# A two-layer hybrid decoder step: the matmul engine's order is fixed by the program, and the small work is cut into stages that leave at counts of big matmuls

## The chip, the cores and the metric

The kernel runs on one core of one Trainium2 chip. Its time is the device time of one execution in microseconds (us); the number to compare is the median of the runs. The engines are named as in the profile: PE (TensorE, matmuls), PEld (PE's weight loads, which run beside its matmuls), DVE (VectorE), ACT (ScalarE), POOL (GpSimd) and SP (SyncE, which here only issues DMAs).

## The reference, cut to what matters

One inference step of two identical layers for 512 prompt tokens and 8 x 4 sample tokens, together 544 token columns, with a model width of 1024:

```python
h = rmsnorm(x, norm1_g) * (1 + mod[:, 1]) + mod[:, 0]      # mod = silu(c) @ w_ada + b_ada, six sections
z = h @ w_in                                               # one projection for four mixers and the gates
yA = pool_mixer(...)       # causal window means, small linear map
yB = retention(...)        # 4 chunks of 128, two pairs of heads
yC = short_conv(...)
yD = rwkv7_mixer(...)      # serial state over the tokens: S = S * w + (S a) b + v k
proj = einsum('btnc,ncd->btnd', stack([yA, yB, yC, yD]), w_br)
x = x + mod[:, 2] * (sum(sigmoid(gates) * proj) @ w_out)
h2 = rmsnorm(x, norm2_g) * (1 + mod[:, 4]) + mod[:, 3]
up = causal_dwconv(h2 @ w_up);  x = x + mod[:, 5] * ((silu(up[:, :2816]) * up[:, 2816:]) @ w_down)
```

After the second layer comes a last rmsnorm. The mixers' states before and after the step are inputs and outputs.

## The kernel before, in words

**Big matmuls.** Activations lie with channels on the 128 partitions and the 544 tokens along the free axis, in two halves of 272. All weights of a layer come as 138 units of 128 x 1024, each loaded by one DMA into a buffer `raw` (three of them) and split into a high part `whi` (ACT, L109) and a remainder `wlo` (DVE, L110). `mm3` makes each product of a 128 x 128 weight tile with 272 tokens of three matmuls (L129, L130, L131); `unit` calls it eight times for one 128-row output of one half, so a unit has 24 big matmuls per half. The results stand in three PSUM buffers `pd`.

**Small work.** Everything else on PE writes one of five PSUM buffers `pm`. It comes from Python generators: `rwkv` (front part, then the scan of 16 chunks of 32 tokens, then the sample tokens and a group norm), `retention` (twice), `ada` (the conditioning `mod`: L191 matmuls on weights that arrive by DMA `in_wada`, layer 0 in `raw` buffers, layer 1 in the large `t4` buffers), and the norms (`rstd_of`, `norm_half`). A chunk of the scan is a serial chain over three engines:

- G: `psG`, L597, then an ACT copy to `gs` (L572);
- S: `psS`, L577, then copies into `Z` by DVE and ACT (L579, L580);
- P: `psP`, L604 (64 x 64 tiles), and `pY`, L608 (128 x 64 tiles), then DVE L616 and L622, which make the next chunk's `Z`.

Every second chunk also has V, `newZ`, L563. `psP` and `pY` do not wait for each other; `pY` feeds only an output.

**What sets the order.** The generators are advanced with `adv` and `tick`, about once per unit of big matmuls, and a `yield` covers a whole chunk. This order in the program is only a priority: the scheduler of the framework orders every engine's queue anew, PE's too, by when it thinks operands are ready. Once built, each engine works through its queue in order and waits at semaphores. The 13248 big and 1836 small matmuls in the built program are the same before and after. Before, PE's queue has 261 stretches of small matmuls, each between big ones (or at an end of the program).

Of the kernel before, what the change touches and what calls it, by code (L numbers as in the profile page):

```python
# [24 lines left out]
NU = 138  # L25
KAPPA = -math.exp(-0.5)
# [16 lines left out]
def tile_hybrid_step(ctx: ExitStack, tc: tile.TileContext, io: dict):  # L43
# [81 lines left out]
    def mm3(ps, w, s, x, first, last):  # L125
        hi, lo = w
        a, b = hi[:, s * 128:(s + 1) * 128], lo[:, s * 128:(s + 1) * 128]
        xh, xl = x
        PE.matmul(ps, lhsT=a, rhs=xh, start=first, stop=False)  # L129
        PE.matmul(ps, lhsT=a, rhs=xl, start=False, stop=False)  # L130
        PE.matmul(ps, lhsT=b, rhs=xh, start=False, stop=last)  # L131

# [47 lines left out]
    def ada(l, sec, ns, load):  # L180
# [3 lines left out]
        nxt = load(0)  # L184
        yield
        for k in range(8):
            raw = nxt
            if k < 7:
                nxt = load(k + 1)
            for n in range(4):  # L190
                PE.matmul(ps[32 * n:32 * n + 32, 0:W], lhsT=sc[:, k, :], rhs=raw[:, W * n:W * n + W], start=(k == 0), stop=(k == 7))  # L191
            yield
        sb = ZR(W)
        S.copy(sb, ps[:, 0:W])
        pt = PM()
# [8 lines left out]
        yield  # L204
# [15 lines left out]
    def adv(g, n=1):  # L220
        for _ in range(n):
            if next(g, StopIteration) is StopIteration:
                return

    bg, ticks = [], [0]

    def tick():
        ticks[0] += 1
        for every, first, g in bg:
            if ticks[0] >= first and ticks[0] % every == 0:  # L230
                adv(g)

# [13 lines left out]
    def rstd_of(accs):  # L246
# [31 lines left out]
    def norm_half(xt, half, acc, sA, shA, hh):  # L278
        c0, c1 = HS[half]
        rs = rstd_of([acc])[0]  # L280
        yield
        for k in range(8):
            u = ZR(HALF)
            V.tensor_tensor(out=u, in0=xk(xt, k)[:, c0:c1], in1=rs, op=MUL)
            modulate(u, k, half, sA, shA, hh)
            yield

    def norm_final(xt, half, acc):
        c0, c1 = HS[half]
        rs = rstd_of([acc])[0]  # L290
        yield
        for k in range(8):
            x = xk(xt, k)[:, c0:c1]
            V.scalar_tensor_tensor(out=x, in0=x, scalar=pars[0][:, P_FG + k:P_FG + k + 1], in1=rs, op0=MUL, op1=MUL)
            if k % 2:
                nc.sync.dma_start(io["o_y"][:, k - 1:k + 1, c0:c1], xt[k // 4][:, k % 4 - 1:k % 4 + 1, c0:c1])
            yield

    def both_halves(run, norm):

        ng = None
        for half in range(2):
            acc = None
            for m in range(8):
                acc = sum_sq(acc, run(m, half))
                if ng:
                    adv(ng, 2 if m else 1)
            if ng:
                adv(ng, 100)
            ng = norm(half, acc)  # L310
# [28 lines left out]
    def ln_bones(src_halves, n, scale, bias, out, floor=None):  # L339

        for c0, c1 in ((0, HALF), (HALF, TOK)):
# [15 lines left out]
    def rwkv(l, za, zb, M, yD):  # L357
# [9 lines left out]
        yield  # L367
        for T in range(5):
            n = 128 if T < 4 else 32
            psu = PM()  # L370
            PE.matmul(psu[0:n, 0:256], lhsT=th[0:65, T * 128:T * 128 + n], rhs=lora[0:65, 0:256], start=True, stop=True)
            S.activation(sig[0:n, T, :], psu[0:n, 0:256], AF.Sigmoid)
        yield
# [6 lines left out]
        yield  # L380
        rss = []
        for p in range(2):
            sq = ZR(TOK)
            S.activation(sq, za[:, 2 + p, :], AF.Square, scale=par[:, P_KK + p:P_KK + p + 1])
            rs = ZR(TOK)
            ln_bones(sq, TOK, None, None, rs, floor=1e-24)
# [5 lines left out]
        yield  # L392
# [6 lines left out]
        yield  # L399
# [39 lines left out]
        yield  # L439
        for T in range(5):  # L440
# [14 lines left out]
            S.copy(BK[:, 4 * T:4 * T + nch, :, :].rearrange("r c p t -> r (c p t)"), psB[:, 0:nch * 128])  # L455
            for c in range(nch):
                for p in range(2):
                    cc = (c * 2 + p) * 64
                    for q in range(2):
                        r = par_rows(q)  # L460
                        PE.matmul(psA[kv_rows(q), cc:cc + 64], lhsT=bkv[r, p, c].rearrange("r w t -> r (w t)"),  # L461
                                  rhs=LG[q][r, 4 * T + c, p, :], start=True, stop=True)
            mc = C_MSK if T < 4 else C_MSS
# [6 lines left out]
            yield  # L470

        for p in range(2):
            for c0, c1 in HS:
                ps = PM()
                PE.matmul(ps[:, :HALF], lhsT=lora[:, 512 + 128 * p:640 + 128 * p], rhs=za[:, 1, c0:c1], start=True, stop=True)
                S.copy(kkb[:, p, c0:c1], ps[:, :HALF])
            rk = ZR(TOK)
            V.tensor_tensor(out=rk, in0=zb[:, p, :], in1=za[:, 2 + p, :], op=MUL)
            for c0, c1 in HS:
                ps = PM()  # L480
                PE.matmul(ps[:, :HALF], lhsT=M["rkb"][:, p, :], rhs=rk[:, c0:c1], start=True, stop=True)
                V.tensor_tensor(out=kkb[:, 2 + p, c0:c1], in0=ps[:, :HALF], in1=zb[:, 2 + p, c0:c1], op=MUL)
        yield

        scr1 = drp.tile([64, 32, 32], F32, tag="scr1", name=nm("scr1"))
        scr2 = drp.tile([64, 16, 2, 32], F32, tag="scr2", name=nm("scr2"))
        for q in range(2):
            r0 = 64 if q == 0 else 0
            for p in range(2):
                nc.sync.dma_start(scr1[(2 * q + p) * 16:(2 * q + p) * 16 + 16].rearrange("c s t -> s c t"),  # L490
                                  LG[q][r0:r0 + 32, 0:16, p, 0:32])
        zaf = za.rearrange("p a b -> p (a b)")
        Nb = zaf[:, 0:1024].rearrange("p (s t) -> p s t", t=32)
        X = zaf[:, 1024:1536].rearrange("p (s t) -> p s t", t=32)
        tm = zaf[:, 1536:2048].rearrange("p (s t) -> p s t", t=32)
        nc.sync.dma_start(Nb[0:64], scr1)
        nc.sync.dma_start(Nb[64:128], scr1)
        nc.sync.dma_start(X, io["xinit"])

# [7 lines left out]
        An = ZR(64)  # L507
        IA = ZR(64)
        I2 = ZR(64)
        psN = PM()  # L510
        XTs = M["xts"]
        for q in range(2):
# [6 lines left out]
                            in1=idb, op=ADD)  # L519
            for p in range(2):  # L520
                PE.matmul(psN[rr, 32 * p:32 * p + 32], lhsT=An[rr, 32 * p:32 * p + 32], rhs=LG[q][rr, 16, p, 0:32],
                          start=True, stop=True)
            V.tensor_tensor(out=I2[rr].rearrange("r (p t) -> r p t", p=2), in0=psN[rr, 0:64].rearrange("r (p t) -> r p t", p=2),
                            in1=idb, op=ADD)
        psX = PM()
        for p in range(2):
            for q in range(2):
                r0 = 64 if q == 0 else 0
                PE.matmul(psX[32 * q:32 * q + 32, 32 * p:32 * p + 32], lhsT=IA[r0:r0 + 32, 32 * p:32 * p + 32],
                          rhs=I2[r0:r0 + 32, 32 * p:32 * p + 32], start=True, stop=True)  # L530
        V.tensor_copy(XTs[0:64].rearrange("r p t -> r (p t)"), psX[0:64, 0:64])
        yield
        for s in range(31):
# [4 lines left out]
            if s in (7, 14, 21):  # L538
                yield
# [8 lines left out]
        yield  # L548
        yield
# [20 lines left out]
        def ginv_sa(psG, xt, Zc):  # L570
            gs = M["pool"].tile([64, 2, 64], F32, tag="gs", name=nm("gs"), bufs=2)
            S.copy(gs.rearrange("r p i -> r (p i)"), psG[0:64, 0:128])  # L572
            psS = PM()
            for p in range(2):
                for q in range(2):
                    r0 = 64 if q == 0 else 0
                    PE.matmul(psS[r0:r0 + 32, 64 * p:64 * p + 64], lhsT=xt(q, p), rhs=gs[32 * q:32 * q + 32, p, :],  # L577
                              start=True, stop=True)
            V.tensor_copy(Zc[0][64:96], psS[64:96, 0:128].rearrange("r (p i) -> r p i", p=2))  # L579
            S.copy(Zc[1][0:32], psS[0:32, 0:128].rearrange("r (p i) -> r p i", p=2))  # L580

        yv = zb[:, 0:2, :]
        Z = newZ(0, 2)
# [3 lines left out]
        for T in range(4):  # L587
            psY = PM()
            pY = psY[:, 0:256].rearrange("p (q x) -> p q x", q=2)
            for c in range(4):  # L590
                ch = 4 * T + c
                if c % 2 == 0:
                    Zn = newZ(ch + 2, 2 if ch < 14 else 1)
                psG = PM()
                for p in range(2):
                    for q in range(2):
                        PE.matmul(psG[32 * q:32 * q + 32, 64 * p:64 * p + 64], lhsT=LG[q][:, ch, p, 0:32],  # L597
                                  rhs=Z[q][:, c % 2, p, :], start=True, stop=True)
                ginv_sa(psG, lambda q, p: XT[32 * q:32 * q + 32, ch, p, :], [Z[0][:, c % 2], Z[1][:, c % 2]])
                psP = PM()  # L600
                for p in range(2):
                    for q in range(2):
                        r = kv_rows(q)
                        PE.matmul(psP[par_rows(q), 64 * p:64 * p + 64], lhsT=BK[r, ch, p, :], rhs=Z[q][r, c % 2, p, :],  # L604
                                  start=True, stop=True)
                for p in range(2):
                    for q in range(2):
                        PE.matmul(pY[par_rows(q), p, 32 * c:32 * c + 32], lhsT=Z[q][:, c % 2, p, :], rhs=LG[q][:, ch, p, 32:64],  # L608
                                  start=True, stop=True)
# [883 lines left out]
```

## Time and profile before

| | us |
|---|---|
| median of 3 runs | 1999.32 |
| lowest and highest run | 1997.35, 1999.36 |
| the profiled execution, its time | 1997.68 |
| its span in the trace | 1995.9 |
| PE busy in it | 1962.4 |
| DVE, ACT, POOL busy | 1047.5, 829.4, 318.8 |

The trace records the fp32 small matmuls as two instructions each, so a group of four in the program is eight in the trace. The recorded duration of a matmul overlaps that of the next one; what a matmul costs is the distance between starts. In rows of the timeline the columns are start in us, duration in us, engine, line, operation, output<-inputs, shape and count, and in brackets the engine's idle time before, with what ended it.

### The profile page before, as it was taken

The numbers are of one execution on the slowest core, as the hardware profiler recorded it, in microseconds if no ns is written. First come the engines' busy times: TensorE is split into PE (matmuls) and PEld (weight loads), VectorE is DVE, ScalarE is ACT, GpSimd is POOL, SyncE is SP. The second block draws the span as 40 slices with busy tenths as digits, with TensorE's granted clock in tenths as the row PEclk, the third lists the DMA queues.
The fourth block names the chain that finished last, engine by engine and source line by source line (L and its number), as shares of the span: only waits on it lengthen the run. The fifth ranks groups of instructions, "written<-read, shape, count | busy, mean of one in ns | idle before, by whom it ended". The sixth has DMA issues, their size and how long they took to land.

```text
span 1995.9 us, 40151 instructions
## 1 busy us (share of the span) xinstructions
PE 1962.4 (98%) x16868; PEld 1850.0 (93%) x16868; DVE 1047.5 (52%) x2017; ACT 829.4 (42%) x1546; POOL 318.8 (16%) x589
## 2 busy tenths in 40 slices
PE   6999999999999999999999999999999999999997
PEld 5999987889999999999999999888999999999997
DVE  4465723443466553555564657344445666555665
ACT  4553322253346442434345533223444565243542
POOL 1110022213001210112202101322120022011210
PEclk9999999999999999999999999999999999999999
DMA  7314423333533443534433223223124132222231
GB/s 308 107 65 128 130 96 129 119 126 114 181 111 107 154 164 128 201 127 160 136 111 95 67 86 88 65 87 111 65 85 160 62 96 86 91 90 85 86 103 46
DMA packets 75557, 227.23 MB, mean 114 GB/s; under 512 B 20208, under 2 KB 23072, under 8 KB 73584
## 3 DMA queue, kind: packets, MB, share of 16 engines
q1 hardware_dynamic: 69872, 210.43, 31.5%
q0 software_dynamic: 3536, 11.53, 1.6%
q10 hardware_dynamic: 1968, 2.69, 0.5%
q8 instruction: 133, 2.18, 0.4%
q14 instruction: 48, 0.39, 0.1%
HBM read 213.33 MB, written 9.06 MB: 111 GB/s over the span
## 4 chain that ended last, share of the span: by engine, by line
PE 95%; DVE 2%; ACT 1%; DMA 1%; issue 0%; ACTq 0%; SPq 0%; DVEq 0%
PE pd L129 28%; PE pd L131 27%; PE pd L130 27%; PE pm L191 2%; PE pm L604 1%; PE pm L608 1%; PE pm L597 1%; PE pm L577 1%; DMA t<-in_wada 1%; PE pm L453 0%; PE pm L563 0%; PE pm L343 0%; PE pm L165 0%; PE pm L461 0%; PE pm L672 0%
## 5 line engine op out<-in xcount | busy, mean ns | idle before, releaser
L129 PE MATMUL pd<-t,whi 128*128 128x272 f32 x4200 | 1227.8, 293 | 5.0 <-ACT t L354 3.5
L131 PE MATMUL pd<-t,wlo 128*128 128x272 f32 x4200 | 1220.6, 291 | 0.0
L130 PE MATMUL pd<-t,whi 128*128 128x272 f32 x4200 | 1214.1, 289 | 0.5 <-DVE t L355 0.5
L129 PEld LDWEIGHTS pd<-t,whi 128*128 128x128 f32 x4200 | 790.2, 188 | 48.4 <-issue 32.6
L130 PEld LDWEIGHTS pd<-t,whi 128*128 128x128 f32 x4200 | 792.5, 189 | 6.7 <-issue 2.6
L131 PEld LDWEIGHTS pd<-t,wlo 128*128 128x128 f32 x4200 | 792.1, 189 | 3.9 <-issue 1.0
L110 DVE TENSOR_TENSOR wlo<-raw,whi 128x1024 fp32r<-128x1024 f32 x262 | 321.8, 1229 | 302.2 <-ACT whi L109 301.4
L109 ACT CAST whi<-raw 128x1024 fp32r<-128x1024 f32 x264 | 276.5, 1049 | 484.0 <-PE pd L130 449.4
L1204 POOL COPY off<-zr 128x18 f32<-128x18 f32 x88 | 76.9, 874 | 570.9 <-ACT zr L1202 570.9
L323 DVE SCALAR_TENSOR_TENSOR t<-pd,mod,t 128x272 f32<-128x272 f32 (+1 forms) x160 | 76.8, 482 | 112.2 <-PE pd L131 111.5
L1024 DVE TENSOR_TENSOR zr<-pd,zr 128x272 f32<-128x272 f32 x96 | 41.7, 437 | 176.3 <-PE pd L131 176.0
L1202 ACT COPY zr<-pd 128x272 f32<-128x272 f32 (+2 forms) x264 | 72.5, 310 | 94.2 <-PE pd L131 94.2
L1039 ACT ACTIVATE zr<-pd 128x272 f32<-128x272 f32 x128 | 50.3, 394 | 138.3 <-PE pd L131 136.2
L1025 POOL TENSOR_TENSOR t<-t,zr 128x272 f32<-128x272 f32 x64 | 73.2, 1160 | 202.1 <-DVE zr L1024 201.8
L953 DVE SCALAR_TENSOR_TENSOR zr<-zr,par,zr 128x560 f32<-128x560 f32 x92 | 73.5, 801 | 5.2 <-ACT zr L952 5.2
L954 DVE SCALAR_TENSOR_TENSOR zr<-zr,par,zr 128x560 f32<-128x560 f32 x92 | 73.5, 801 | 2.9
L952 ACT ACTIVATE zr<-zr,par 128x560 f32<-128x560 f32 x92 | 70.5, 766 | 8.1 <-ACT zr L1202 0.7
L355 DVE TENSOR_TENSOR t<-zr,t 128x544 fp32r<-128x544 f32 (+1 forms) x96 | 54.0, 581 | 30.9 <-ACT t L354 30.1
L240 ACT ACTIVATE zr<-t 128x272 f32<-128x272 f32 (+1 forms) x72 | 32.1, 454 | 86.5 <-DVE t L323 56.6
L354 ACT CAST t<-zr 128x544 fp32r<-128x544 f32 (+1 forms) x96 | 48.9, 531 | 43.8 <-DVE zr L1215 42.4
L1200 POOL COPY zr<-sff 128x16 f32<-128x16 f32 x88 | 41.0, 476 | 0.7 <-DMA sff<-in_s_ffn 0.4
L1211 ACT ACTIVATE zr<-zr 128x560 f32<-128x560 f32 x44 | 29.6, 672 | 24.9 <-DVE zr L954 24.9
(286 smaller groups left out, 1666.0 us busy)
## 6 DMA issues: line engine op xcount, KB each, us to landing
raw<-in_wst SPq DMA_DIRECT2D x276, 512.0 KB, 3.5
t<-in_wada SPq DMA_DIRECT2D x32, 1024.0 KB, 7.8
raw<-in_wada SPq DMA_DIRECT2D x32, 512.0 KB, 3.5
zr<-in_rope POOLq DMA_DIRECT2D x16, 272.0 KB, 3.1
t<-in_xT SPq DMA_DIRECT2D x4, 544.0 KB, 7.0
zr<-zr ACTq DMA_DIRECT2D x32, 68.0 KB, 4.1
t<-in_xT SPq DMA_DIRECT2D x2, 1088.0 KB, 8.5
xs<-t SPq DMA_DIRECT2D x2, 1088.0 KB, 4.4
```

The lines of the kernel that those rows point to most:

```text
L109: S.copy(hi, raw)
L110: (G if (l, u) in ((0, 1), (0, 2)) else V).tensor_tensor(out=lo, in0=raw, in1=hi, op=SUB)
L129: PE.matmul(ps, lhsT=a, rhs=xh, start=first, stop=False)
L130: PE.matmul(ps, lhsT=a, rhs=xl, start=False, stop=False)
L131: PE.matmul(ps, lhsT=b, rhs=xh, start=False, stop=last)
L323: V.scalar_tensor_tensor(out=x[:, c0:c0 + npc], in0=ps[:, :npc], scalar=gate[:, m, 0:1], in1=x[:, c0:c0 + npc], op0=MUL, op1=ADD)
L952: S.activation(cv, u[:, 0:560], AF.Copy, scale=wcol(0))
L953: V.scalar_tensor_tensor(out=cv, in0=u[:, 1:561], scalar=wcol(1), in1=cv, op0=MUL, op1=ADD)
L954: V.scalar_tensor_tensor(out=cv, in0=u[:, 2:562], scalar=wcol(2), in1=cv, op0=MUL, op1=ADD)
L1025: (V if last else G).tensor_tensor(out=a[:, c0:c1], in0=a[:, c0:c1], in1=gs, op=ADD)
L1202: pad_evac(lambda o, i, sl: S.copy(o, i), u, ps, half, 2)
L1204: G.tensor_copy(off[:, 22 * s + j], u[:, 512:562].rearrange("p (x t) -> p x t", t=2)[:, 0:25:3, :])
```

## The change

The program is built with PE under a manual schedule: PE's queue is the order in which the program issues its matmuls. DVE, ACT, POOL and SP are still ordered by the scheduler. The ticks go; instead `mm3` counts its matmuls and calls `slot` after each three. Each generator is entered with `spawn`, and each `yield n` says after how many more big matmuls its next stage is due; a negative number marks a stage without matmuls, which leaves as soon as it is due. When any stage with matmuls is due (and its slack is over), all that are due leave together. `finish` issues what is left of a generator.

```diff
@@ mm3
         PE.matmul(ps, lhsT=b, rhs=xh, start=False, stop=last)
+        nmm[0] += 3
+        slot()
+    def spawn(g, after=0, slack=0):
+        e = {"due": nmm[0] + abs(after), "pe": after >= 0, "g": g, "slack": slack}
+        gens.append(e)
+        return e
+    def slot():
+        for e in [e for e in gens if not e["pe"] and nmm[0] >= e["due"]]:
+            step(e)
+        if any(e["pe"] and nmm[0] >= e["due"] + e["slack"] for e in gens):
+            for e in [e for e in gens if e["pe"] and nmm[0] >= e["due"]]:
+                step(e)
@@ ada: ns weight blocks per stage (ns = 1 in layer 0, 2 for layer 1)
-        nxt = load(0)
-        yield
-        for k in range(8):
-            raw = nxt
-            if k < 7:
-                nxt = load(k + 1)
...
+        raws = [load(k) for k in range(ns)]
+        yield 60
+        for k in range(0, 8, ns):
+            for i in range(ns):
...
+            if k + ns < 8:
+                raws.extend(load(k + ns + i) for i in range(ns))
+                yield 30 * ns
@@ rstd_of
+        yield 18
+        for d in ds:
             ps = PM()
             PE.matmul(ps[:, 0:HALF], lhsT=ones[0:n, :], rhs=d[0:n, 0:HALF], start=True, stop=True)
@@ both_halves
-            ng = norm(half, acc)
+            ng = spawn(norm(half, acc), 24)
@@ rwkv, the scan: D_G, D_S, D_P = 12, 12, 18
+            S.copy(gs.rearrange("r p i -> r (p i)"), psG[0:64, 0:128])
...
+            yield D_G
+            psS = sa_of(lambda q, p: XT[32 * q:32 * q + 32, ch, p, :], gs)
+            if c % 2 == 0:
+                Zn = newZ(ch + 2, 2 if ch < 14 else 1)
+            sa_out(psS, [Z[0][:, c % 2], Z[1][:, c % 2]])
+            yield D_S
...
-                yield
-                if c % 2:
-                    Z = Zn
+            yield D_P
@@ the layer
-        rw = rwkv(l, za, zb, M, yD)
-        adv(rw, 1)
-        bg.append((1, 0, rw))
-            bg.append((1, 8, ada_all(0, range(2, 6), 1)))
+        rw = spawn(rwkv(l, za, zb, M, yD), -3)
+            spawn(ada_all(0, range(2, 6), 1), -30, 900)
...
-            bg.append((2, 0, ada_all(l + 1, range(6), 2)))
+            ada_next = spawn(ada_all(l + 1, range(6), 2), -60)
@@ kernel
     with tile.TileContext(nc) as tc:
-        tile_hybrid_step(tc, io)
+        with tc.manual_schedule(engines={mybir.EngineType.PE}):
+            tile_hybrid_step(tc, io)
```

The other stages of `rwkv` get distances of 6 to 48, those of `retention` 24; a retention starts only when its inputs are there and the scan is done. Some statements move between neighbouring stages: the squares of `rwkv` to its first stage, the load of `s_wkv` to chunk 13, its L642 matmuls to chunk 14, the load of `s_ret` to the start of `retention`. PE's queue now has 188 stretches of small matmuls.

PE's queue in the scan of layer 0, within the gates of the pooling branch. `pm_3115` is `psP` of a chunk, `pm_2725` is `pY`, `pd` is a gate unit. Before:

```order
L130 MATMUL pd_3149<-t_40_193,whi_3025 128x272
L604 MATMUL pm_3115<-z_2726,t_174_1379 64x64
L608 MATMUL pm_2725<-t_172_1377,z_2726 64x32
L131 MATMUL pd_3149<-t_38_191,wlo_3026 128x272
L604 MATMUL pm_3115<-z_2727,t_174_1379 64x64
L604 MATMUL pm_3115<-z_2726,t_174_1379 64x64
L604 MATMUL pm_3115<-z_2727,t_174_1379 64x64
L608 MATMUL pm_2725<-t_173_1378,z_2727 64x32
L608 MATMUL pm_2725<-t_172_1377,z_2726 64x32
L608 MATMUL pm_2725<-t_173_1378,z_2727 64x32
L129 MATMUL pd_3149<-t_38_191,whi_3025 128x272
```

A big matmul stands in the middle of the stage P. The stage is cut in two in this way in 25 of the 32 chunks of both layers, and G in 6. Now (L654 and L658 are the old L604 and L608), in the same gates:

```order
L132 MATMUL pd_2538<-t_119_997,wlo_1921 128x272
L654 MATMUL pm_2542<-z_2315,t_155_1175 64x64
L654 MATMUL pm_2542<-z_2316,t_155_1175 64x64
L654 MATMUL pm_2542<-z_2315,t_155_1175 64x64
L654 MATMUL pm_2542<-z_2316,t_155_1175 64x64
L658 MATMUL pm_2386<-t_153_1173,z_2315 64x32
L658 MATMUL pm_2386<-t_154_1174,z_2316 64x32
L658 MATMUL pm_2386<-t_153_1173,z_2315 64x32
L658 MATMUL pm_2386<-t_154_1174,z_2316 64x32
L130 MATMUL pd_2538<-t_119_997,whi_1920 128x272
```

P is in one piece, and so it is in all 32 chunks.

PE's queue where `pool_linear` makes the second half of `yA` (layer 0). `pm_2837` and `pm_2840` are its results, `t_309` is `yA` (first half, channels of `pool_linear(0)`), `t_38` and `t_40` are `h`. Before:

```order
L1097 MATMUL pm_2837<-zr_2625,pw_598 128x272
L1097 MATMUL pm_2840<-zr_2625,pw_598 128x272
L129 MATMUL pd_2845<-t_309_2433,whi_2436 128x272
L130 MATMUL pd_2845<-t_309_2433,whi_2436 128x272
L131 MATMUL pd_2845<-t_309_2433,wlo_2437 128x272
L129 MATMUL pd_2854<-t_309_2433,whi_2436 128x272
L130 MATMUL pd_2854<-t_309_2433,whi_2436 128x272
L131 MATMUL pd_2854<-t_309_2433,wlo_2437 128x272
L597 MATMUL pm_2863<-z_2708,t_172_1377 32x64
```

After these come three more matmuls of G, six matmuls of a gate unit (`t_38`, `t_40`), and only then those that read the second half of `yA`. Now:

```order
L1162 MATMUL pm_3072<-zr_2825,pw_600 128x272
L1162 MATMUL pm_3075<-zr_2825,pw_600 128x272
L130 MATMUL pd_3080<-t_329_2577,whi_2580 128x272
L131 MATMUL pd_3080<-t_329_2577,whi_2580 128x272
L132 MATMUL pd_3080<-t_329_2577,wlo_2581 128x272
L654 MATMUL pm_3084<-z_2850,t_155_1175 64x64
```

Three big matmuls and one stage P follow `pool_linear`; the next big matmul reads the second half of `yA`. Layer 1 has the same order there.

More of the change, by code (lines that the diff above doesn't have):

```diff
@@ L25 @@
 NU = 138
+D_G, D_S, D_P = 12, 12, 18
 KAPPA = -math.exp(-0.5)
@@ L469, in rwkv @@
                     in1=cst[r, mc:mc + 64].unsqueeze(1).broadcast_to([64, 2 * nch, 64]), op=MUL)
-            yield
+            if T == 3:
+                scr1 = drp.tile([64, 32, 32], F32, tag="scr1", name=nm("scr1"))
+                for q in range(2):
+                    r0 = 64 if q == 0 else 0
+                    for p in range(2):
+                        nc.sync.dma_start(scr1[(2 * q + p) * 16:(2 * q + p) * 16 + 16].rearrange("c s t -> s c t"),
+                                          LG[q][r0:r0 + 32, 0:16, p, 0:32])
+            if T < 4:
+                yield 44
+        rks = []
         for p in range(2):
[L473 to L476, printed above, removed]
             rk = ZR(TOK)
             V.tensor_tensor(out=rk, in0=zb[:, p, :], in1=za[:, 2 + p, :], op=MUL)
[L479 to L498, printed above, removed]
+            rks.append(rk)
+        yield 20
         psA2 = PM()
@@ L506, in rwkv @@
                           start=True, stop=True)
[L507 to L511, printed above, removed]
+        for p in range(2):
+            for c0, c1 in HS:
+                ps = PM()
+                PE.matmul(ps[:, :HALF], lhsT=lora[:, 512 + 128 * p:640 + 128 * p], rhs=za[:, 1, c0:c1], start=True, stop=True)
+                S.copy(kkb[:, p, c0:c1], ps[:, :HALF])
+        An, IA, I2 = M["sinv"]
         for q in range(2):
@@ L519, in rwkv @@
                             in1=idb, op=ADD)
+        scr2 = drp.tile([64, 16, 2, 32], F32, tag="scr2", name=nm("scr2"))
+        zaf = za.rearrange("p a b -> p (a b)")
+        Nb = zaf[:, 0:1024].rearrange("p (s t) -> p s t", t=32)
+        X = zaf[:, 1024:1536].rearrange("p (s t) -> p s t", t=32)
+        tm = zaf[:, 1536:2048].rearrange("p (s t) -> p s t", t=32)
+        nc.sync.dma_start(Nb[0:64], scr1)
+        nc.sync.dma_start(Nb[64:128], scr1)
+        nc.sync.dma_start(X, io["xinit"])
+        yield 24
+        psN = PM()
+        XTs = M["xts"]
+        for q in range(2):
+            r0 = 64 if q == 0 else 0
+            rr = slice(r0, r0 + 32)
             for p in range(2):
@@ L582, in rwkv @@
         yv = zb[:, 0:2, :]
+        psX = PM()
+        for p in range(2):
+            for q in range(2):
+                r0 = 64 if q == 0 else 0
+                PE.matmul(psX[32 * q:32 * q + 32, 32 * p:32 * p + 32], lhsT=IA[r0:r0 + 32, 32 * p:32 * p + 32],
+                          rhs=I2[r0:r0 + 32, 32 * p:32 * p + 32], start=True, stop=True)
+        V.tensor_copy(XTs[0:64].rearrange("r p t -> r (p t)"), psX[0:64, 0:64])
         Z = newZ(0, 2)
@@ new lines, in rwkv @@
+            G.tensor_tensor(out=Pn, in0=Pt, in1=db, op=MUL)
+            if c == 3:
+                S.copy(yv[:, :, T * 128:T * 128 + 128], pY)
+            if c % 2:
+                Z = Zn
+            if ch == 14:
+                psG0 = PM()
+                g0v = psG0[:, 0:128].rearrange("r (p w b t) -> r p w b t", p=2, w=2, t=DT)
+                for p in range(2):
+                    for b in range(NB):
+                        for q in range(2):
+                            r = par_rows(q)
+                            PE.matmul(g0v[r, p, :, b, :], lhsT=P0[p][r, 64 * b:64 * b + 64],
+                                      rhs=LG[q][r, 16, p, :].rearrange("r (w b t) -> r w b t", w=2, t=DT)[:, :, b, :],
+                                      start=True, stop=True)
+                g0 = ZR(128)
+                S.copy(g0, psG0[:, 0:128])
+                g0s = g0.rearrange("r (p w x) -> r p w x", p=2, w=2)
@@ L676, in rwkv @@
             G.dma_start(io["o_wkv_s"][l, :, p], P0[p])
-        yield
-        rss = []
+        M["scan_done"] = True
+        yield 12
+        rss = [ZR(TOK) for _ in range(2)]
         for p in range(2):
@@ L728, in retention @@
             sms.append(sm)
-        yield
+        yield 24
+        ps = PM()
+        pv = PM()
+        for q in range(2):
+            r = par_rows(q)
+            PE.matmul(ps[32 * q:32 * q + 32, 0:32], lhsT=rt[r, 1, SEQ:TOK], rhs=rt[r, 0, SEQ:TOK], start=True, stop=True)
+        for i, src in enumerate((2, 1)):
+            for q in range(2):
+                r = par_rows(q)
+                PE.matmul(pv[32 * q:32 * q + 32, 64 * i:64 * i + 64], lhsT=rt[r, src, SEQ:TOK], rhs=ident[r, 64 * q:64 * q + 64],
+                          start=True, stop=True)
         pst = PM()
@@ L734, in retention @@
                           start=True, stop=True)
+        sms_s = ZR(32)
+        V.tensor_tensor(out=sms_s[0:64], in0=ps[0:64, 0:32], in1=cst[0:64, C_RETS:C_RETS + 32], op=MUL)
+        vks = ZR(128)
+        S.copy(vks[0:64], pv[0:64, 0:128])
         V.tensor_copy(Sb[:, 1], pst[:, 0:64])
@@ L776, in retention @@
                           start=True, stop=True)
-        S.copy(o[:, SEQ:TOK], psC[:, 0:32])
-        V.tensor_tensor(out=o[:, SEQ:TOK], in0=psO2[:, 0:32], in1=o[:, SEQ:TOK], op=ADD)
-        Vx = ZR(512)
-        V.tensor_tensor(out=Vx[0:64].rearrange("r (b e) -> r b e", b=NB),
-                        in0=vks[0:64, 0:64].unsqueeze(1).broadcast_to([64, NB, 64]),
-                        in1=cst[0:64, C_BM:C_BM + 8].unsqueeze(2).broadcast_to([64, NB, 64]), op=MUL)
+        for q in range(2):
+            r = par_rows(q)
+            PE.matmul(psO2[r, 0:32], lhsT=vks[32 * q:32 * q + 32, 0:64], rhs=sms_s[32 * q:32 * q + 32, :], start=True, stop=True)
         psX = PM()
@@ L800, in retention, with retentions @@
         split_hilo(o, yB[0][:, 2 * p, :], yB[0][:, 2 * p + 1, :])
-        yield
+    def retentions(l, rts, M, yB):
+        while not (M.get("ret0") and M.get("scan_done")):
+            yield -6
+        yield 18
+        yield from retention(l, 0, rts[0], M, yB)
+        while not M.get("ret1"):
+            yield -6
+        yield 18
+        yield from retention(l, 1, rts[1], M, yB)
     def pad_evac(fn, dst, ps, half, pad):
@@ L840, in tile_hybrid_step @@
     afs = [ada_first(k) for k in range(8)]
+    rss = []
+    rg = rstd_of([acc[:, c0:c1] for c0, c1 in HS], rss)
+    next(rg)
     next(afs[0])
-    rss = rstd_of([acc[:, c0:c1] for c0, c1 in HS])
+    next(rg, None)
     hh = new_hh()
@@ L876, in tile_hybrid_step @@
         M["xts"] = mp.tile([64, 2, 32], F32, name=nm("xts"))
+        sinv = mp.tile([128, 3, 64], F32, name=nm("sinv"))
+        M["sinv"] = [sinv[:, i] for i in range(3)]
         M["dec"] = mp.tile([128, 2, 24], F32, name=nm("dec"))
```

334 lines of the change are left out of this document (151 added, 183 removed).

## The prediction

> **What bounds the kernel now.** I read the page first: busy time by engine and the chain that ended last.
>
> ```profile
> PE 1962.4 (98%) x16868; PEld 1850.0 (93%) x16868; DVE 1047.5 (52%) x2017; ACT 829.4 (42%) x1546; POOL 318.8 (16%) x589
> ...
> PE 95%; DVE 2%; ACT 1%; DMA 1%; issue 0%; ACTq 0%; SPq 0%; DVEq 0%
> ```
>
> PE is the bound: 98% busy, 95% of the chain. Only two things can move the end: what PE's own queue costs in its order, and new waits in it. The next view is PE's timeline in a stretch of big matmuls (start, duration).
>
> ```profile
> 599.77 0.29 PE L129 MATMUL pd<-t,t 128*128 128x272 f32 x1
> ...
> 607.92 0.29 PE L131 MATMUL pd<-t,wlo 128*128 128x272 f32 x1
> ```
>
> 65 steps lie between these starts: 8.15/65 = 0.125 us each. The 13248 big matmuls take 1661 us in this way, before and after. The rest, some 335 us, is the small work with the seams around it, and the head and tail. The small matmuls keep their number. So the change can save seams alone, and it is priced by them: a stretch costs the start of the second big matmul after it, less the start of the last one before it, less 0.125 for each step of a big matmul in between (two steps without anything in the way). The second is taken because the first one after a stretch is late too.
>
> **Stages kept in one piece.** A stage P of before, cut in two by a big matmul:
>
> ```profile
> 269.95 0.28 PE L130 MATMUL pd<-t,whi 128*128 128x272 f32 x1
> 270.16 0.33 PE L604 MATMUL pm<-z,t 64*64 64x64 f32 x2
> 270.42 0.30 PE L608 MATMUL pm<-t,z 128*64 128x32 f32 x2
> 270.65 0.39 PE L131 MATMUL pd<-t,wlo 128*128 128x272 f32 x1
> 270.97 0.44 PE L604 MATMUL pm<-z,t 64*64 64x64 f32 x6
> ...
> 271.93 0.29 PE L130 MATMUL pd<-t,whi 128*128 128x272 f32 x1
> ```
>
> And one that stood whole:
>
> ```profile
> 248.26 0.29 PE L131 MATMUL pd<-t,wlo 128*128 128x272 f32 x1
> 248.48 0.45 PE L604 MATMUL pm<-z,t 64*64 64x64 f32 x8
> 248.86 0.42 PE L608 MATMUL pm<-t,z 128*64 128x32 f32 x8
> ...
> 249.44 0.29 PE L129 MATMUL pd<-t,whi 128*128 128x272 f32 x1
> ```
>
> Cut: 271.93 - 269.95 = 1.98, less three steps, 1.605. Whole: 249.44 - 248.26 = 1.18, less two, 0.93. The cut costs 0.675 us, and the order has it in 25 chunks and no more in any: 25 x 0.675 = -16.9 us. Ends: -12 (0.5 each, if the other cuts fall better) to -20.
>
> **Stages that leave together.** PE's queue has 261 stretches before and 188 now: 73 fewer, of which the 25 are counted. What a merger saves, from two stages alone and the same two together:
>
> ```profile
> 1306.33 0.29 PE L131 MATMUL pd<-t,wlo 128*128 128x272 f32 x1
> 1306.54 0.64 PE L563 MATMUL pm<-cst,t 64*32 64x64 f32 x16
> ...
> 1307.35 0.28 PE L130 MATMUL pd<-t,whi 128*128 128x272 f32 x1
> ...
> 245.38 0.29 PE L131 MATMUL pd<-t,wlo 128*128 128x272 f32 x1
> 245.59 0.42 PE L597 MATMUL pm<-z,t 128*32 128x64 f32 x8
> ...
> 246.17 0.29 PE L130 MATMUL pd<-t,whi 128*128 128x272 f32 x1
> ...
> 255.73 0.28 PE L131 MATMUL pd<-t,wlo 128*128 128x272 f32 x1
> 255.94 0.64 PE L563 MATMUL pm<-cst,t 64*32 64x64 f32 x16
> 256.51 0.42 PE L597 MATMUL pm<-z,t 128*32 128x64 f32 x8
> ...
> 257.09 0.29 PE L130 MATMUL pd<-t,whi 128*128 128x272 f32 x1
> ```
>
> Alone 1.02 - 0.25 = 0.77 and 0.79 - 0.25 = 0.54, together 1.36 - 0.25 = 1.11: 0.20 saved. For the remaining 48 stretches, -9.6 us. The 0.675 of a cut is more, since there the tile's shape changes twice more; a merger of whole stages saves no such change, so the nearer row is 0.20. Ends: -5 (0.1 each) to -19 (0.4).
>
> **The wait that exists in the scan.** PE waits once in a G of before:
>
> ```profile
> 342.70 0.27 PE L597 MATMUL pm<-z,t 128*32 128x64 f32 x2 [1.81 <-DVE z L622]
> ```
>
> DVE was held by other work there. The new distances may or may not put a G at such a place: -1, ends -1.8 and 0.
>
> **New waits in the scan.** PE now meets each next stage after 12, 12 and 18 big matmuls: 1.50, 1.50 and 2.25 us. If the copies between are not done, PE stands still, big matmuls and all, as nothing can overtake. What the copies take, and what can stand ahead of them on DVE and ACT (busy, mean ns):
>
> ```profile
> L109 ACT CAST whi<-raw 128x1024 fp32r<-128x1024 f32 x264 | 276.5, 1049 | 484.0 <-PE pd L130 449.4
> L572 ACT COPY gs<-pm 64x128 f32<-64x128 f32 x34 | 8.8, 258 | 15.8 <-PE pm L597 13.0 <-PE pm L655 2.4
> L110 DVE TENSOR_TENSOR wlo<-raw,whi 128x1024 fp32r<-128x1024 f32 x262 | 321.8, 1229 | 302.2 <-ACT whi L109 301.4
> L579 DVE COPY z<-pm 32x128 f32<-32x128 f32 x34 | 9.8, 289 | 37.6 <-PE pm L577 37.1
> L622 DVE TENSOR_TENSOR z<-pt,dec 64x128 f32<-64x128 f32 x60 | 20.0, 333 | 1.7
> ```
>
> G to S is the ACT copy, 0.26, at worst behind a whole cast: 1.31 of 1.50. S to P is the DVE copy, 0.29, at worst behind a whole L110: 1.52 of 1.50. P to G is L616, of the same kind as L579, and L622: 0.29 + 0.33 + 1.23 = 1.85 of 2.25, and the L608 matmuls give 0.35 more. So only the worst case of S to P misses by itself, and the hops between engines add some tenths. L110 fills 321.8 of 1996 us, 16%. 34 visits x 16% x about half a us is 2.7, much of it in the slack: +2 us. Ends: 0, and 0.25 us at each of some 100 visits, +25.
>
> **A new wait in the pooling branch.** The order has three big matmuls and one P between `pool_linear` and the first reader of its result, in both layers. The chain of before (PE, ACT, DVE):
>
> ```profile
> 243.83 1.08 PE L1097 MATMUL pm<-zr,pw 128*128 128x272 f32 x4
> ...
> 246.03 0.65 ACT L354 CAST t<-zr 128x544 fp32r<-128x544 f32 x1
> ...
> 246.71 0.72 DVE L355 TENSOR_TENSOR t<-zr,t 128x544 fp32r<-128x544 f32 x1 [0.51 <-ACT t L354]
> ```
>
> From L1097's start to the cast's end it is 2.85 us (246.68), to the remainder's 3.60. L1097 takes some 0.7 of PE (the next start was 244.54), three big matmuls 0.4 and P 0.93: PE asks after about 2.0 to 2.1. It waits 0.7 to 0.8 for the cast and up to 0.5 more for the remainder, two matmuls later: 1.2 us in each layer, +2.4. Ends: 0 (another order on ACT) and +4.
>
> **Conditioning of layer 1.** During the FFN of layer 0, 12 stages each read two loads of 1 MB, now issued 60 big matmuls ahead (7.5 us); before, PE took one load per 13 us. The landing of such loads between 885 and 1000 us:
>
> ```profile
> DMA to landing us min/median/max: 5.7/5.8/9.2
> ```
>
> Usually 1.7 us are left, at the slowest 1.7 are missing. SP's queue is in order: a load that waits for its buffer delays the `raw` loads behind it, but these keep 49 big matmuls (6 us) or more of slack in the order. +1, ends 0 and 12 x 1.7 = +20.
>
> **Head and norms.** At the head, and where a norm ends:
>
> ```profile
> 13.28 1.93 PE L165 MATMUL pm<-t,sc 128*32 128x128 f32 x32 [13.28 <-DMA t<-in_wada]
> ...
> 29.30 1.05 PE L129 MATMUL pd<-t,whi 128*128 128x272 f32 x3 [3.55 <-ACT t L354]
> ...
> 1034.04 0.36 PE L129 MATMUL pd<-t,t 128*128 128x272 f32 x1 [1.40 <-DVE zr L327]
> ```
>
> The first norm's matmuls no longer stand behind these 1.93 us of L165, but DVE has more of the conditioning ahead of the work that ends the 3.55: -1, ends -4 and +1. At the later norms the second step is 18 big matmuls after the first, where it came after 8 to 14: with the one wait of 1.40 as the measure, +0.6, ends 0 and +3.
>
> The trace shows a price of long waits, the clock granted at the head (busy us and count, clock):
>
> ```profile
> 29.00:31.50 2.50, 2.19 (x9) 2.20 (x10) 2.50 (x12) 2.50 (x7) 0.00 (x0) 0.50 1.01 419
> 31.50:34.00 2.50, 2.50 (x19) 2.23 (x21) 1.22 (x4) 1.32 (x4) 0.00 (x0) 0.50 1.00 391
> ```
>
> After 3.55 us of idle PE, a big matmul takes 2.19/9 = 0.24 instead of 0.125, for 5 us: about 20 x 0.115 = 2.3 us on top of the wait. [...]
>
> **Sum**, against the profiled execution's own 1997.7: -16.9 - 9.6 - 1 (wait) + 2 + 2.4 + 1 - 1 (head) + 0.6 = -22.5, so 1975 us. The median of the runs is 1.6 above that execution, within their own spread of 2.0; I leave it.
>
> **Rivals.**
> - *Many short waits eat half or more of the gain.* PE in program order waits at a good part of the 100 scan visits by some tenths, or at the 12 conditioning stages by up to 1.7. For it: the program order does not know when DVE and ACT are free. Against it: the worst cases above fit but one. 12 us of waits more give 1987, all 12 x 1.7 = 20 give 1995.
> - *Slower.* The scan's serial chain becomes the bound: each visit waits. Place: G, S and P, some 100 visits. It decides from 24.5/100, about 0.25 us each beyond the 2 us counted; at 0.4 each it is 1975 + 38 = 2013. For it: 0.25 is less than one L579. Against it: G to S and P to G have 0.2 to 0.7 us of slack even behind the longest blocker.
> - *The clock falls.* If a conditioning stage waits over 3.5 us, it costs 3.5 + 2.3 = 5.8, in 12 stages 70: 2045. It needs landings of 11 us, where the slowest shown was 9.2.
> - *More gain.* Mergers at 0.4 (-9.6 more) and no new waits: 1960.
>
> **How the numbers follow.** The forecast (1964 to 1984) 0.72; half or more of the gain eaten 0.15, of which 0.04 within 0.2% of before (4 us, about what a measurement of this kernel tells from no change); slower by the scan 0.05, by the clock 0.02; more gain 0.06. That makes faster 0.89, same 0.04, slower 0.07. The range for 8 in 10 reaches from 1963 to 1989: below, the ends of the two savings and the head; above, +14 of the scan's or the conditioning's ends.
>
> **What would show it.** Right: the stretches L654 and L658 in one piece at about 0.93 us; PE's idle time before L577's successor and before L597's small, some 1.2 before the gate matmul behind `pool_linear` in both layers. Wrong: idle of PE behind DVE or ACT in the scan that sums to over 10 us; PE waits on `in_wada`; a clock under 1 in the FFN; stretches that cost as much per stage as before though fewer.

## The result and the profile after

The changed kernel takes 1970.01 us in the median of four runs (1967.96 to 1970.54), beside 1998.34 us for the kernel before (1996.68 to 1999.36) on the same chip. The ratio is 0.9857, with a 95% interval of 0.984 to 0.9874: faster by 1.4%. The forecast was 1975, within 1963 to 1989. The span of the profiled execution falls from 1995.9 to 1968.8 us, by 27.1.

From the page of the kernel after, the busy times and the chain that ended last:

```profile
PE 1924.9 (98%) x16868; PEld 1834.8 (93%) x16868; DVE 1046.1 (53%) x2017; ACT 814.8 (41%) x1531; POOL 313.3 (16%) x589
...
PE 91%; DVE 4%; ACT 2%; DMA 2%; issue 1%; ACTq 0%; POOL 0%; DVEq 0%; POOLq 0%
```

PE does the same 16868 recorded matmuls in 37.5 us less busy time, and the chain passes more often through DVE, ACT and DMA than before (8% instead of 4%). So PE has fewer seams and more waits. The waits of PE, summed (engine, line, what it waited for, total us, times, longest):

```profile
PE pm L272 <- DVE zr L262: 14.9, 2, 13.1
PE pm L201 <- ACT t L198: 6.6, 2, 5.2
PE pm L286 <- DVE zr L279: 3.0, 4, 1.1
PE pm L477 <- DVE zr L458: 2.8, 2, 1.4
PE pd L130 <- ACT t L373: 1.8, 3, 0.7
PE pm L636 <- DVE z L672: 1.6, 2, 0.8
PE pd L130 <- DVE zr L346: 1.4, 1, 1.4
PE pm L362 <- ACT zr L743: 1.2, 1, 1.2
...
PE pd L131 <- DVE t L374: 0.8, 2, 0.4
PE pm L654 <- DVE z L610: 0.6, 2, 0.3
```

The first line is mainly the start of the program (13.1 us, where before L165 waited 13.3 for `in_wada`), and the 5.2 of the second stands before the first big matmul. Between the head and the last norm no wait is longer than 1.4 us, and none is for `in_wada`. For the accounts below, each stretch of small matmuls is priced as in the prediction, and all of them are summed from the 19th big matmul on (what stands before it is called the head):

| | before | after |
|---|---|---|
| first big matmul, start | 29.3 | 31.35 |
| 19th big matmul, start | 35.3 | 37.0 |
| stretches after that, us | 258, 280.5 | 185, 250.1 |
| PE's idle time within them | 2.1 | 11.3 |
| the stretches without it | 278.4 | 238.8 |

The seams are cheaper by 39.6 us; 9.2 us of that go into new waits within the stretches, and the head loses 1.7. That leaves -28.7 against the measured -27.1; the other 1.6 us lie between big matmuls and are not placed singly.

A whole P after, in the timeline:

```profile
280.89 0.29 PE L132 MATMUL pd<-t,wlo 128*128 128x272 f32 x1
281.10 0.45 PE L654 MATMUL pm<-z,t 64*64 64x64 f32 x8
281.48 0.43 PE L658 MATMUL pm<-t,z 128*64 128x32 f32 x8
281.84 0.39 PE L130 MATMUL pd<-t,whi 128*128 128x272 f32 x1
282.06 0.29 PE L131 MATMUL pd<-t,whi 128*128 128x272 f32 x1
```

282.06 - 280.89 - 0.25 = 0.92, the price that the whole P had before. 28 of the 32 stand alone like this, with a median of 0.93.

### The profile page after: what moved, and what is told of

Its sections match the earlier page's. It is cut to its first block, busy times and chain, and to the rows that moved or that the text cites. A ratio compares the mean times of both kernels' runs of the same rounds, so it can differ in the third digit from the quotient of the medians.

```text
span 1968.8 us, 40136 instructions
## 1 busy us (share of the span) xinstructions
PE 1924.9 (98%) x16868; PEld 1834.8 (93%) x16868; DVE 1046.1 (53%) x2017; ACT 814.8 (41%) x1531; POOL 313.3 (16%) x589
## 4 chain that ended last, share of the span: by engine, by line
PE 91%; DVE 4%; ACT 2%; DMA 2%; issue 1%; ACTq 0%; POOL 0%; DVEq 0%; POOLq 0%
PE pd L130 28%; PE pd L132 27%; PE pd L131 26%; PE pm L220 2%; DMA raw<-in_wst 1%; ACT whi L110 1%; DVE wlo L111 1%; PE pm L654 1%; PE pm L636 1%; PE pm L605 1%; DMA zr<-zr 1%; PE pm L658 1%; PE pm L593 0%; PE pm L477 0%; PE pm L484 0%
## 5 line engine op out<-in xcount | busy, mean ns | idle before, releaser
L1094 POOL TENSOR_TENSOR t<-t,zr 128x272 f32<-128x272 f32 x64 | 68.9, 1093 | 119.5 <-DVE zr L1093 119.4
L1022 ACT ACTIVATE zr<-zr,par 128x560 f32<-128x560 f32 x92 | 70.2, 765 | 17.1 <-DVE zr L1047 9.6
L610 DVE COPY z<-pm 32x128 f32<-32x128 f32 x34 | 9.8, 289 | 69.7 <-PE pm L605 69.4
L262 DVE TENSOR_TENSOR zr<-zr,zr 128x272 f32<-128x272 f32 (+1 forms) x63 | 29.9, 475 | 20.0 <-ACT zr L259 19.3
```

The lines of the kernel that those rows point to most:

```text
L1022: S.activation(cv, u[:, 0:560], AF.Copy, scale=wcol(0))
L1094: (V if last else G).tensor_tensor(out=a[:, c0:c1], in0=a[:, c0:c1], in1=gs, op=ADD)
```

## Experiments

Theory: what pays is that stages stay whole and leave together, so that PE changes between big and small work less often; PE in program order only adds waits. Rivals: the program's order itself is what pays; or a seam costs the same wherever it falls. All medians are compared with the kernel after (1970.0) and with the kernel before, which ran at 1997.9 to 2000.0 in these comparisons.

**P cut again.**

```diff
+            pq = [(0, 0), (0, 1), (1, 0), (1, 1)]
+            for part in (pq[:1], pq[1:]):
...      # L654 of part, then L658 of part
+                if len(part) == 1:
+                    yield 3
```

> The new kernel with each stage P cut again, as before: one L654 and one L658, three big matmuls, then the other three of each; 30 more stretches of small matmuls than the new kernel (218 to 188). By the prediction's first term (0.675 us for each cut) 32 cuts cost 21.6 us: about 1991. Rival: a cut costs no more than any other seam (0.20 by the merger's row, 0.45 if the whole gain is spread evenly over the 73 stretches): 6 to 14 us, 1976 to 1984.

2003.25 us, ratio to before 1.0028 (1.0018 to 1.0038): all of the gain and more is gone, and the time is 12 us above the 1991 expected. The price by rows is the forecast one: the parts cost 0.917 and 0.684 (medians of 30), whole 0.93, so 0.67 for each cut and 20.1 us for 30. The span grew by 32.1. Another 4.8 us are idle time of PE (21.4 after the head, where it was 16.6): the scan is 3 big matmuls later in each of 16 chunks, and its end is met by PE's `finish`:

```profile
PE pm L728 <- DVE zr L714: 5.3, 3, 4.0
```

And 17.1 us of the run have a granted clock of 0.50, where it was 3.4 (the last section): 13.7 us more. In the stretch at 0.50 of the kernel after, a big matmul starts every 0.227 us (ten steps from 332.58 to 334.85) instead of every 0.125, so by my estimate the 13.7 are worth at most half, 6.8. Together 31.7.

**The stages, but the scheduler on PE.**

```diff
-        with tc.manual_schedule(engines={mybir.EngineType.PE}):
-            tile_hybrid_step(tc, io)
+        tile_hybrid_step(tc, io)
```

> The new stages, but PE's queue ordered by the scheduler again: the manual schedule alone is taken out. The order has 196 stretches (188 in the new kernel, 261 before) and three stages P cut. If seams are what pays, it is within 5 us of the new kernel's 1970: 8 stretches more cost 2 to 4, the three cuts 2, the head's 1.7 comes back, some of the 8 us of new waits go. Rival: the program's order on PE is what pays: most of the 28 us are lost, 1985 or more.

1963.51 us (1962.03 to 1963.64), ratio 0.9825 (0.981 to 0.984): 6.5 us faster than the changed kernel. The intervals of the two ratios only touch at 0.984, but the traces say the same (span 1961.8 beside 1968.8). The stages bring the whole gain; the manual order takes some back. PE's waits here, without that of the start:

```profile
PE pd L130 <- ACT t L373: 5.1, 1, 5.1
PE pm L477 <- DVE zr L458: 2.8, 2, 1.4
PE pd L130 <- DVE zr L346: 2.7, 2, 1.7
PE pm L286 <- DVE zr L279: 1.1, 1, 1.1
```

The waits in the scan, in the pooling branch and for L286 are gone (its 1.1 is the one at the end of the program, as before): 9.8 us of idle time after the head instead of 16.6, and the 19th big matmul starts at 34.9 instead of 37.0. Its eight more stretches cost 3.0 us beside idle time (241.8 to 238.8); 2.0 of this are three stages P that its order cuts again, 0.67 each.

**No merging.**

```diff
-            for e in [e for e in gens if e["pe"] and nmm[0] >= e["due"]]:
-                step(e)
+            pend.extend(...)          # all that are due
+        if pend:
+            step(pend.pop(0))         # one after each three big matmuls
```

> The new kernel, but stages that are due together leave one after another, three big matmuls apart: 34 more stretches (222 to 188), no stage cut. By the prediction's merger term (0.20 each) +7: 1977. By 0.34, what the new trace shows for a conditioning block with a G (0.976 together, 0.77 and 0.54 alone before), +12: 1982. If all gain beyond the cuts is put on the 48 mergers (0.45), +15: 1985.

1979.87 us (1976.8 to 1982.75), +9.9. Without idle time its stretches cost 247.1 instead of 238.8 us: 8.3 for 34, 0.24 each on average. The rest is idle time, 18.9 after 16.6. So the row of the prediction (0.20) was a fair price for a merger.

**Program order alone.** The kernel before, with the manual schedule put around it.

> The kernel before with PE in program order and nothing else changed: 128 stretches, but G, S and P of a chunk stand behind one another without big matmuls between. Savings of 133 stretches by 0.3 to 0.45: -40 to -60. Waits: G to S and S to P in 32 chunks, each the copy and the hops, 0.6 to 1.5 us with a cast or a remainder ahead, +40 to +95, and the conditioning blocks. Prediction's slower rival shown at its place: 1990 to 2050, PE idle behind L572 and L579. Rival: the program's order pays by itself: 1970.

2159.12 us, ratio 1.081 (1.0794 to 1.0827), slower than the range expected. Its waits:

```profile
PE pm L577 <- ACT gs L572: 34.6, 34, 4.3
PE pm L264 <- DVE zr L260: 18.0, 9, 3.2
PE pm L604 <- DVE z L579: 15.6, 32, 1.1
```

The scan costs 50 us here, as expected; the whole idle time after the head is 118.0 us (8.3 before). 191.1 us inside the run are at a clock of 0.50. Without stages that leave room, program order is a loss, and the slower rival of the prediction is real: it is the distances that keep it away.

**P cut between whole pairs.** As the first, with `pq[:2], pq[2:]`.

> As the kernel with P cut, but the cut falls between whole pairs: two L654 and two L658, three big matmuls, then the other two of each. Two matmuls of a pair lie on different quarters of TensorE's array; in the traces such neighbours start 7 ns apart, and a cut after the first one parts a pair of L654 and a pair of L658. If the parted pairs make up most of a cut's 0.67 us, a cut costs about 0.3 here, and the kernel stands some 11 us (30 x 0.37) below the other one's 2003: 1992. If the seam and the change of tile shape make it, it costs 0.6 or more again: 2000 or above.

1998.1 us (1993.85 to 2002.05), ratio 0.9995 (0.9984 to 1.0007) where the first had 1.0028; the profiled span is 7.1 us shorter (1993.8). Two parts of 0.696 (median of 60) against 0.93: 0.46 for a cut. Neither expected value is met: of the 0.67, 0.21 go away when the cut leaves pairs of matmuls together, and 0.46 stay. What the 0.46 consist of (the seam, the changes of tile shape) was not separated.

**Short distances.** `D_G, D_S, D_P = 6, 6, 9`.

> The new kernel with the scan's distances halved, D_G, D_S, D_P = 6, 6, 9: 0.75, 0.75 and 1.13 us. The prediction's slower rival at work: G to S is the end of the matmuls (0.3), a copy of 0.26 and the hops, some 0.1 to 0.3 us too long for the distance, more with a cast ahead; S to P the same; P to G with two DVE steps of 0.29 and 0.33 about 0.3. In 34 visits each 15 to 25 us of PE waiting behind L603, L610 and L672: 1985 to 1995. Rival: the distances have reserve, and waits stay at a few us: 1970 to 1975.

2000.48 us, ratio to before 1.0012 (1.0003 to 1.0022): the gain is gone, and the time is above both expected values. But the waits grew only from 16.6 to 26.0 us; the largest group behind the head, and one of its waits:

```profile
PE pm L636 <- DVE z L672: 10.4, 6, 2.7
```

```profile
246.50 0.84 PE L636 MATMUL pm<-z,t 128*32 128x64 f32 x7 [2.71 <-DVE z L672]
```

PE's clock in slices around it (columns: width, busy us and count of PE, PEld, DVE, ACT, POOL, then clock, DMA share, GB/s):

```profile
242.40:245.80 3.40, 1.40 (x12) 1.18 (x9) 3.25 (x9) 0.00 (x0) 1.07 (x1) 1.00 0.47 154
245.80:249.20 3.40, 2.70 (x20) 1.75 (x21) 0.90 (x5) 0.26 (x1) 0.00 (x0) 0.51 0.02 5
249.20:252.60 3.40, 3.40 (x26) 2.73 (x24) 0.29 (x1) 0.64 (x2) 0.00 (x0) 0.50 0.51 154
```

After a slice in which PE was busy for 1.40 of 3.40 us, two slices run at half clock. There are 44.4 us of this, 41 more than in the kernel after: at most 20.5 us lost, and with 9.4 of waits this covers the 30.7 of the span.

**Two waits mended.** The manual schedule starts behind the head, and `pool_linear(1)` goes out between the halves of its gate unit.

```diff
+    ctx.enter_context(tc.manual_schedule(engines={mybir.EngineType.PE}))
     for l in range(L):
...
+                    if mid and m == 1 and half == 0:
+                        mid()
...
-        gates(lambda: yA, False, False, [lambda: pool_linear(0), lambda: pool_linear(1)])
+        gates(lambda: yA, False, False, [lambda: pool_linear(0)], lambda: pool_linear(1))
...
-        with tc.manual_schedule(engines={mybir.EngineType.PE}):
-            tile_hybrid_step(tc, io)
+        tile_hybrid_step(tc, io)
```

> The new kernel with two of its waits mended: the manual schedule begins only after the head (the scheduler orders PE until the first units are done), and pool_linear(1) is issued 24 big matmuls earlier, between the halves of its gate unit. The head should give back 2.0 us (the 18th big matmul at 34.9 instead of 37.0), the two waits for L373 and L374 2 x 1.13: 4.3 together, 1966. If the waits only move to the next place, the time stays at 1969 to 1970.

1964.29 us (1962.87 to 1965.43), ratio 0.9829 (0.9812 to 0.9845), -5.7. The span fell by 7.4: the 19th big matmul starts at 35.8 (-1.2), the waits of the pooling branch are gone, and idle time after the head is 13.5 (-3.1). The slice at half clock inside the run is gone as well, worth at most 1.7.

**The scan's front part later, under the scheduler.** `yield 60` for `yield 48` behind the first `products`.

> The new stages with the scheduler on PE (1963.5), and 60 instead of 48 big matmuls between the first products of rwkv and L477, which waited 1.39 us for DVE in each layer. -2.8 if the wait goes and the later scan still ends in time: 1960.7. If the scan's end is pushed into the place where it is needed, 1963 to 1968.

1963.31 us (1961.64 to 1964.63): no change against 1963.51. L477 waits no more, but new waits stand elsewhere:

```profile
PE pd L130 <- DVE zr L1047: 2.4, 2, 1.2
PE pd L130 <- ACT t L1188: 1.5, 2, 1.2
```

Idle time after the head is 11.0 (9.8). Of the versions tried, those with the scheduler on PE (1963.3 and 1963.5) and the one with the manual order behind the head (1964.3) are the fastest, and cannot be told apart.

**Quarters apart.** The loops over `q` and `p` at L654 and L726 are exchanged.

> The new kernel with two loops turned: L654 and L726 go through both pairs of heads for one quarter of the array, then for the other, so that fewer neighbours lie on different quarters. If such neighbours run side by side, and this is what L726 (L672 of before) gained, its eight recorded matmuls in a layer take up to twice 1.8 us, 3.5 (two in the middle may still overlap), and L654's part of P gets longer by 0.1 to 0.2. Rival: L672 was slow for another reason (its wait for zr), and nothing changes: 1.8 us in a layer, P 0.93.

One run, 1974.32 us. The row of the groups for L726 reads the same in the kernel after and in this one:

```profile
L726 PE MATMUL pm<-zr,t 64*64 64x512 f32 x16 | 3.9, 602 | 0.0
```

P's median is 0.936 beside 0.930. The first expectation fell and its rival held: the order within these stages made no difference to their price here. The time is 4.3 us above that of the kernel after; its trace has 10.2 us at half clock inside the run instead of 3.4, worth at most 3.4, and one run tells no more.

**Small matmuls three times.** `for p in [0, 1] * 3` at L685; the results are written over with the same values.

> The new kernel with the 32 matmuls L685 (64 x 64 by 8 columns) issued three times over in each layer: 6 us without a big matmul, PE never idle. It tells what lowers the granted clock in the middle of the run. If low activity of the array is enough, the clock goes to 0.50 during or after these matmuls in both layers, for 3.4 us or more. Rival: only idle time of PE lowers it, and then there is no new slice at 0.50 there. Cost: 8 us for the matmuls, and by the first theory 2 to 5 more.

One run, 1983.85 us. PE in layer 0 (timeline), and the slices after:

```profile
329.57 7.21 PE L685 MATMUL pm<-t,zr 64*64 64x8 f32 x192
```

```profile
330.00:333.40 3.40, 3.40 (x124) 3.40 (x120) 0.39 (x2) 0.00 (x0) 0.80 (x2) 1.00 0.27 82
333.40:336.80 3.40, 3.40 (x69) 3.38 (x65) 0.00 (x0) 0.00 (x0) 0.00 (x0) 0.51 0.02 5
336.80:340.20 3.40, 3.40 (x15) 3.40 (x16) 0.00 (x0) 0.27 (x1) 0.00 (x0) 0.50 0.00 0
```

PE was busy for all 3.40 us of the first slice, and the next two have 0.50. In layer 1, where L685 runs from 1307.07 to 1315.34, the clock falls too, for 10.2 us. PE was not idle ahead of either fall.

## Why the prediction was right, and where its steps were not

- *Stages kept in one piece*, -16.9: held. 25 cuts cost 1.02 + 0.58 before and 0.93 now, 0.67 each, -16.7; the first experiment gave the same 0.67 with the sign turned. That it is the tile's shape that makes a cut dearer than a merger was not shown.
- *Stages that leave together*, -9.6, ends -5 to -19: mis-sized. The remaining 48 stretches brought 39.6 - 16.7 = 22.9 us, more than the end. The price of a merger was near (0.24 on average in the experiment). The fault was to count all 48 as mergers of whole stages. Among them were more cuts: six of G, at 0.42 + 0.54 against 0.54, 0.42 each, 2.5 together. Conditioning blocks of layer 1 in pairs cost 2.05 instead of 2 x 1.19, 0.33 saved in each of 12, 3.9 together. And a stage of which I saw nothing, the sample tokens' L672. Before, in layer 0:

```profile
393.51 1.69 PE L672 MATMUL pm<-zr,t 64*64 64x512 f32 x4
...
395.72 1.07 PE L672 MATMUL pm<-zr,t 64*64 64x512 f32 x2
...
397.12 1.07 PE L672 MATMUL pm<-zr,t 64*64 64x512 f32 x2
```

and after (L726):

```profile
351.32 1.93 PE L726 MATMUL pm<-zr,t 64*64 64x512 f32 x8
```

  The same eight records take 1.93 us, where four alone took 1.69. In the program of before each matmul came right after the DVE operation that makes its own operand; in the trace the first two started 0.62 us apart, and the other two stood alone in the queue. Now all operands are made a stage earlier, and two at a time start within 7 ns. Both layers: 7.2 us before, 3.7 after, -3.5.

  These three make 9.9 us. The other 13.0 fall on some 30 stretches, 0.43 each, more than the 0.24 of the experiment. Fourteen of them are a conditioning block that now leaves with a G (0.977 together, 0.764 and 0.545 alone, 0.33 saved), 4.6 together; the remaining 8.4 are not placed singly.
- *The wait that exists in the scan*, -1: it went away whole, -1.8.
- *New waits in the scan*, +2: 2.2 (1.6 for L636, 0.6 for L654). The size was luck. The prediction spread its 2 us over 34 visits, with one cast or remainder ahead, and had only S to P missing its distance. The waits stand at one place in each layer, S to P by 0.3 us and, larger, P to G by 0.8, where DVE has a string of the pooling branch's own operations (L1134 to L1153) ahead of L666 and L672, which make G's operand. In layer 0:

```profile
235.76 0.29 DVE L610 COPY z<-pm 32x128 f32<-32x128 f32 x1
236.08 0.86 DVE L1135 TENSOR_TENSOR t<-t 64x676 f32<-64x676 f32 x1
...
239.31 0.29 DVE L666 TENSOR_TENSOR pt<-pm,pn 128x128 f32<-128x128 f32 x1
239.64 0.17 DVE L1153 TENSOR_TENSOR zr<-zr,t 64x15 f32<-64x15 f32 x1
239.84 0.78 DVE L672 TENSOR_TENSOR z<-pt,dec 64x128 f32<-64x128 f32 x2
```

  At all other visits of the scan PE does not wait.
- *Pooling branch*, +2.4: 2.3. The two waits of layer 0, as forecast one for the cast and one for the remainder, and in layer 1 the same within 0.01:

```profile
265.16 0.39 PE L130 MATMUL pd<-t,whi 128*128 128x272 f32 x1 [0.72 <-ACT t L373]
...
265.97 0.39 PE L131 MATMUL pd<-t,whi 128*128 128x272 f32 x1 [0.41 <-DVE t L374]
```

  Each time PE starts 0.05 us after the operation it waited for has ended (at 265.11 and 265.91), where the prediction had some tenths for the hops in the scan.
- *Conditioning of layer 1*, +1: none. The step that a pair's loads go out 60 big matmuls ahead of their use was wrong: SP is still ordered by the scheduler, and between 560 and 720 us its queue waits at these loads nine times (17.2 us) for the L220 matmuls that read the ones before.

```profile
573.07 0.43 SPq L244 DMA_DIRECT2D t<-in_wada  x1
590.36 4.26 SPq L244 DMA_DIRECT2D t<-in_wada  x5
```

```profile
610.50 1.90 PE L220 MATMUL pm<-t,sc 128*32 128x512 f32 x16
```

  The first pair was issued 37 and 20 us ahead of its use; over the 24 loads it is 9 us at least. The landing was wrong as well, and the other way: from issue to landing these loads (with two of layer 0) took

```profile
DMA to landing us min/median/max: 3.5/8.3/15.4
```

  where the prediction went by 5.8, and 9.2 for the slowest. Seven of the 24 took over 11 us, the condition of its clock rival, and the one with least to spare landed 0.5 us before its use. That nothing waits is two errors that met.
- *Head*, -1: +1.7, the wrong sign, past the end of +1. PE's queue has L201 ahead of the first big matmul, and waits there:

```profile
28.53 1.02 PE L201 MATMUL pm<-cst,t 128*128 128x9 f32 x4 [5.18 <-ACT t L198]
29.49 1.94 PE L196 MATMUL pm<-t,sc 128*32 128x128 f32 x32
31.35 0.60 PE L130 MATMUL pd<-t,whi 128*128 128x272 f32 x1
```

  I priced what stands ahead of L201 on PE, not what stands ahead of its operand: ACT's copy L198 was queued behind activations that need DVE's longer first run (16 products in one piece, 5.87 us).
- *Norms*, +0.6: L286 waits at three places inside the run, 1.9 us together, where the old L264 did not; the 1.38 for L346 was there before, and a second wait of 0.51 beside it went. L477 (2.8 in both layers) and L362 (1.2) were not in the sum: stages whose distances I had not checked.
- *Rivals.* Short waits and the scan's chain did not decide, since the distances hold but at one place in each layer; halved, they would have cost the gain. Of "more gain" the saving came true (22.9 us, where mergers at 0.4 would give 19.2), but not its condition that no new waits come.
- *Clock.* The prediction gave a price in clock only to a wait of 3.5 us, from the 3.55 at the head. With the halved distances the clock fell to 0.50 at a wait of 2.71 us, and with the tripled matmuls without one: see below. It cost the forecast nothing, since before and after have one slice of 3.4 us at 0.50 each behind the head.

The sum came out 5 us high because errors of both signs met: 13 us too little for the merged stages, and on the other side about 7 us too little for waits and the head, and the 1.6 not placed.

## What to carry to other kernels

Where one engine is the bound and does large and small work in turn, count the changes between them in its queue, and give the program stages that are whole and late enough; that brought the gain here, under either order (1970.0 and 1963.5 us beside 1998). An order that is fixed by hand on one engine while the others are still scheduled turns each misplaced operand into a wait of that engine (118.0 us of idle time after the head instead of 8.3, with program order alone), so check each stage's distance against the chain that makes its operand, with the queue of the engine that runs it. And when stages are regrouped, look for matmuls of part of the array that waited for operands of their own: side by side, those of the sample tokens cost 3.7 us here instead of 7.2.

## What the runs showed of the hardware

The granted clock fell to 0.50 also without a long wait, for 3.4 us or two or three times that. In the kernel after it does so once between the head and the end of the run, behind a slice in which PE was busy throughout, 2.0 us of it with matmuls of 8 columns:

```profile
329.00:332.40 3.40, 3.40 (x87) 3.27 (x86) 0.96 (x3) 0.27 (x1) 1.03 (x2) 1.00 0.25 69
332.40:335.80 3.40, 3.40 (x26) 3.15 (x28) 0.00 (x0) 0.00 (x0) 0.00 (x0) 0.50 0.05 18
```

The tripled matmuls show it in both layers (6.8 and 10.2 us), and the halved distances show it after a slice with 2.0 us of idle PE. The slice ahead of such a fall holds 6 big matmuls in the kernel before (the fall at 1441.2), 7 in the kernel after, 9 with the halved distances and none with the tripled matmuls, where 27 fill one (427.9 to 431.3 of the kernel after). So it came behind slices with few big matmuls, whether PE waited in them or ran small ones; what in them brings it about was not separated. Few big matmuls alone did not do it: a slice of 3.4 us at 424.5 of the kernel after has none, only small matmuls of 4 to 512 columns, and the clock stayed at 1.00; it also stayed there around the same 64 matmuls of 8 columns in layer 1 (1301.5). It was paid on top of the waits: with the halved distances these grew by 9.4 us and the span by 30.7, with 41 us more at 0.50.

The matmuls of 64 x 64 tiles in L726, issued together, started two within 7 ns and the next two 0.43 to 0.48 us later; the eight records of a layer took 1.93 us. With the loops exchanged they took 1.94 (354.00 of that run), 602 ns each on average in both. What in the array brings this about was not separated.
